# A fifth buffer for the unsplit weights of a two-layer decoder trunk, with three tiles moved into shared buffers

## The chip, the core and the metric

The kernel runs as one program on one core of a Trainium2 chip. Its time is the device time of one execution in microseconds (us). Five engines run side by side, each through its own instructions in a fixed order, and wait for each other through semaphores: TensorE (PE, matrix products into PSUM, with weight loads shown apart as PEld), VectorE (DVE), ScalarE (ACT), GpSimd (POOL) and SyncE (SP). DMA transfers are issued from the instruction streams of SP, POOL and ACT. An instruction whose semaphore isn't there yet holds up everything behind it on the same engine.

## The reference, cut to what matters

The input is 512 positions of 1024 channels, all numbers float32. Two layers follow each other; each is a mixer and a gated feed-forward block (FFN), both added to the residual `h`.

```python
def gated_conv_ffn(x, w_gate, w_up, conv_w, conv_b, w_down):
    g = jnp.einsum('bsd,df->bsf', x, w_gate)
    g = causal_dwconv3(g, conv_w) + conv_b
    up = jnp.einsum('bsd,df->bsf', x, w_up)
    return jnp.einsum('bsf,fd->bsd', jax.nn.silu(g) * up, w_down)

def reference(x, ...):
    h = x
    for layer in range(2):
        xn = rms_norm(h, norm_mix[layer])
        if layer == 0:   # projections to 2048 channels; gated convolution, causal pooling
            mix = concat(short_gated_conv(...), multiscale_pool(z, w_pool, pool_scale))
            h = h + mix @ w_out_even
        else:            # gelu(xn @ w_in_odd) = u, v; mixing of positions in chunks of 128
            h = h + chunked_spatial_gating(u, v, sgu_norm, w_spatial, b_spatial) @ w_out_odd
        hn = rms_norm(h, norm_ffn[layer])
        h = h + gated_conv_ffn(hn, ...)        # 1024 -> 2816 -> 1024
    return rms_norm(h, final_norm)
```

## The kernel before

**Products and their weights.** PE multiplies float32 data in three products (`mm3`, L133 to L135): both factors are split into a rounded part `hi` and a rest `lo`, and hi by hi, hi by lo and lo by hi are added in PSUM. So every block of weights goes through three tiles. The first is `raw`, 128 x 1024 float32 (512 KB), which a DMA on SP's queue fills from memory; then come `whi` and `wlo`, which the products read. `parts` (L125) makes them with one ACT copy (L128) and one DVE subtraction (L129). `summed` (L116) makes `wlo` without DVE: ACT writes minus the raw block into it (L120) and a DMA issued by POOL adds the raw block in place (L121). All raw blocks share the pool tag `raw` with four buffers; `whi` and `wlo` have six each. A raw buffer can be loaded again when all its readers are through, a `summed` block's DMA among them.

**The FFN.** The 2816 hidden channels are 22 tiles of 128, worked off in pairs f = 0, 2, 4, ... 20. From f = 4 on, `both(f)` computes the gate and the up projection of two tiles by a scheme with seven half-size products in place of eight, which needs sums of weight blocks. It takes four raw blocks, here called `g0`, `u0`, `g1` and `u1` of the pair: gate and up weights of the first and the second half of the 1024 input channels. L653, L654, L659 and L660 (DVE) form the sums `s12` and `s34` from them; L653 reads both halves (`g0` and `g1`, or `u0` and `u1`). Lines 633 and 634 split `a11` and the sums; `g1` and `u1` go through `summed`. PE then runs 14 groups of 12 products (L624) in a written order (L695 to L697); their results leave PSUM by ACT copies (L682) and DVE additions (L687, L692) into `rows` and `kept`. L692 after product 7 also frees the bank that product 3 then adds into. The convolution follows (`conv`: L505 on ACT, two L507 on DVE into a tile `c`), then silu (L513), the product with the up projection (L703, L704, L707) and the split of the activation into `a_hi` (L247) and `a_lo` (L249). After the pairs listed in `PARTS` (f = 0 and 2; 4; 6 and 8; 10 and 12; 14 and 16; 18 and 20) a down projection adds to the output: `project` with blocks `d` in layer 0 (results taken by L292), blocks `dn` in layer 1 (L922). It too takes four raw blocks per part. "Boundary 8 to 10" below is the place where the down projection of the part that ends with pair 8 is followed by pair 10.

**What sets the order.** The source says which work there is and what depends on what. A scheduler puts the instructions of each engine in order when the program is built, from modelled durations, and hands out the buffers; so a changed buffer count also moves instructions. On the chip the order is fixed. SP issues the raw loads in the order in which the blocks are used: `g0`, `u0`, `g1`, `u1` of a pair, then the blocks of the next pair or of the down projection. With four buffers, the load of a block waits for the readers of the block four places ahead of it in that list; and a load that waits holds up those behind it in SP's queue.

**The tiles that the change moves.** `wpl` holds the pooling weights of mixer 0 (L425), `g_bc` the norm gain of the spatial unit of mixer 1 (L751), and `c` the convolution of the FFN (L504, two buffers of its own). The tag `sq` of the pool `tp` (two buffers) holds squares for the norms. `fin`, the last norm's gain, already shares the tag `raw` (L899).

Of the kernel before, what the change touches and what calls it, by code (L numbers as in the profile page):

```python
# [8 lines left out]
F32 = mybir.dt.float32  # L9
# [6 lines left out]
P = 128  # L16
D = 1024
S = 512
# [12 lines left out]
def tile_trunk(ctx: ExitStack, tc: tile.TileContext, x, norm_mix, norm_ffn, final_norm,  # L31
# [8 lines left out]
    wp = ctx.enter_context(tc.tile_pool(name="wp", bufs=1))  # L40
    tp = ctx.enter_context(tc.tile_pool(name="tp", bufs=2))
# [3 lines left out]
    def mm_bank(name):  # L45
        return ps_mm.tile([P, 512], F32, tag="mm", name=name)
# [59 lines left out]


    def fetch(src, a, b, name):
        raw = wp.tile([P, a, b], F32, tag="raw", bufs=4, name=f"raw_{name}")
        nc.sync.dma_start(raw, src)  # L110
        return raw, a, b, name

    def weights(src, a, b, name):
        return parts(*fetch(src, a, b, name))
# [108 lines left out]
    def newton(ms, n, name, r):  # L223


        sd = work("sd", n, name)
        nc.scalar.activation(sd, ms, AF.Sqrt)
        nc.vector.reciprocal(r, sd)
        nc.vector.tensor_tensor(ms, ms, r, ALU.mult)
        nc.vector.scalar_tensor_tensor(ms, ms, -0.5, r, op0=ALU.mult, op1=ALU.mult)  # L230
# [71 lines left out]
    def in_fetch(name, w, c0, k, n):  # L302
        return fetch(w[k * P : (k + n) * P, c0 : c0 + 512].rearrange("(k p) c -> p k c", p=P),
                     n, 512, f"{name}_{k}")
# [28 lines left out]
    def mixer0():  # L333
        nonlocal prm0
        w = w_in_even[0]
        with tc.tile_pool(name="m0", bufs=1) as mp:
# [85 lines left out]
            in_group("z", w, 1536, True, z_done, 2, zchunks, ahead)  # L422
            prm0 = params0()

            wpl = mp.tile([P, 4, P], F32, name="wpl")  # L425
            nc.sync.dma_start(wpl, w_pool[0].rearrange("g c d -> c g d"))
            wpl_hi = mp.tile([P, 4, P], F32R, name="wpl_hi")
            wpl_lo = mp.tile([P, 4, P], F32R, name="wpl_lo")
# [59 lines left out]
    class Ffn:  # L488
# [12 lines left out]

        def conv(self, t, ft):
            ap, prm, n = self.ap, self.prm, f"{self.layer}_{ft}"
            c = ap.tile([P, S], F32, tag="c", bufs=2, name=f"c{n}")  # L504
            nc.scalar.activation(c, t[:, 0:S], AF.Copy, scale=prm("cf", ft))  # L505
            for i in (1, 2):
                nc.vector.scalar_tensor_tensor(c, t[:, i : S + i], prm("cf", i * NF + ft), c,  # L507
                                               op0=ALU.mult, op1=ALU.add)
            return c
# [9 lines left out]
        def pair_weights(self, f, order, by_dma=""):  # L519

            ch = {}
            for key, half in order:
                name = f"{key}{self.layer}_{f}_{half}"
                raw = wp.tile([P, 4, 2 * P], F32, tag="raw", bufs=4, name=f"raw_{name}")
                w = (w_ffn_gate if key == "g" else w_ffn_up)[self.layer][:, f * P : (f + 2) * P]
                w = w.rearrange("(h k p) c -> p h k c", h=2, p=P)
                for h_ in range(2):
                    nc.sync.dma_start(raw.rearrange("p (k h) c -> p h k c", h=2)[:, h_],
                                      w[:, h_, 2 * half : 2 * half + 2])
                ch[key, half] = (summed if key in by_dma else parts)(raw, 4, 2 * P, name)  # L530
            return ch
# [216 lines left out]
    def mixer1(norm):  # L748
        w = w_in_odd[0]
        with tc.tile_pool(name="m1", bufs=1) as mp:  # L750
            g_bc = mp.tile([P, 1, D], F32, name="g_bc")  # L751
            nc.scalar.dma_start(g_bc, sgu_norm.rearrange("(o l) d -> o l d", o=1)
                                .to_broadcast([P, 1, D]))
            ws = mp.tile([P, NK, P], F32, tag="v", bufs=4, name="ws")
# [117 lines left out]
    def ffn1(norm):  # L872
        with tc.tile_pool(name="f1", bufs=1) as ap:
            def sums(kp):
                return [cp.tile([P, 2, HALF], F32R, tag=f"h{k}", name=f"t23_{k}")
                        for k in (kp, kp + NP)]

            ffn = Ffn(1, prm1, norm, ap, sums)
            acts = ffn.acts
            y = [ap.tile([P, D], F32, name=f"y{t}") for t in range(NT)]  # L880
            ssf = ap.tile([P, NT, PAD], F32, name="ssf")[:, :, :2]

            def turn_residual(t, half):
                ps = mm_bank(f"hT{t}_{half}")
                for i in range(4):
                    nc.tensor.transpose(ps[:, i * P : (i + 1) * P],
                                        h[half * 4 + i][:, t * P : (t + 1) * P], ident)
                nc.scalar.copy(y[t][:, half * 512 : (half + 1) * 512], ps)

            def before(i, j):  # L890
                if i < 2:
                    turn_residual(j, i)

            for groups, a, b in PARTS:
                for f in groups:
                    ffn.hidden(f, before=before)
                last = b == NF
                if last:
                    fin = wp.tile([P, D], F32, tag="raw", bufs=4, name="fin")  # L899
                    nc.scalar.dma_start(  # L900
                        fin, final_norm.rearrange("(o d) -> o d", o=1).to_broadcast([P, D]))
                    root = small[:, 2:3]
                    nc.scalar.activation(root, eps, AF.Sqrt)
                ch = {}
                for ft in range(a, b):
                    ch[ft] = weights(w_ffn_down[1][ft * P : (ft + 1) * P, :]
                                     .rearrange("(k p) c -> p k c", p=P), 1, D, f"dn1_{ft}")

                def lhs(ft, j):
                    ts_ = slice((j // 2) * P, (j // 2 + 1) * P)  # L910
                    return acts[ft][0][:, ts_], acts[ft][1][:, ts_]

                def rhs(ft, j):
                    c = slice((j % 2) * 512, (j % 2 + 1) * 512)
                    return ch[ft][0][:, 0, c], ch[ft][1][:, 0, c]

                yf = {}

                def done(j, ps):
                    t, half = j // 2, j % 2  # L920
                    dst = y[t][:, half * 512 : (half + 1) * 512]
                    nc.vector.tensor_tensor(dst, ps, dst, ALU.add)  # L922
                    if not last:
                        return
                    sq = tp.tile([P, S], F32, tag="sq", name=f"sqf{j}")
                    ss = ssf[:, t, half : half + 1]
                    nc.scalar.activation(sq, dst, AF.Square, accum_out=ss)
                    yf[half] = ap.tile([P, S], F32, tag="s", bufs=3, name=f"yf{j}")
                    nc.vector.tensor_tensor(yf[half], dst, fin[:, half * 512 : (half + 1) * 512],
                                            ALU.mult)  # L930
                    if half == 0:
                        nc.vector.tensor_scalar(ss, ss, 1.0 / D, EPS, op0=ALU.mult, op1=ALU.add)
                        return
                    ms = ssf[:, t, 0:1]
                    nc.vector.scalar_tensor_tensor(ms, ss, 1.0 / D, ms, op0=ALU.mult, op1=ALU.add)
                    r = tp.tile([P, LINE], F32, tag="rc", name=f"rc_fin{t}")[:, :1]
                    newton(ms, 1, f"fin{t}", r)
                    nc.vector.tensor_scalar(ms, ms, 1.5, None, op0=ALU.add)
                    for c in range(2):
                        cs = slice(c * 512, (c + 1) * 512)  # L940
                        nc.vector.tensor_scalar(y[t][:, cs], yf[c], r, ms,
                                                op0=ALU.mult, op1=ALU.mult)
                        nc.sync.dma_start(out[t * P : (t + 1) * P, cs], y[t][:, cs])

                group8(f"dn{a}", list(range(a, b)), lhs, rhs, 4, done)

    def group8(name, ks, lhs, rhs, tail, on_done):
        banks = {}
        head = max(0, len(ks) - tail)
        order = [(i, j) for i in range(head) for j in range(8)]  # L950
        order += [(i, j) for j in range(8) for i in range(head, len(ks))]
        for i, j in order:
            if j not in banks:
                banks[j] = mm_bank(f"{name}_{j}") if j < 7 else aux_bank(f"{name}_{j}")
            mm3(banks[j], lhs(ks[i], j), rhs(ks[i], j), i == 0, i == len(ks) - 1)
            if i == len(ks) - 1:
                on_done(j, banks[j])

    n = mixer0()
    n = ffn0(n)  # L960
    n = mixer1(n)
    ffn1(n)


# [28 lines left out]
```

## Time and profile before

| | |
|---|---|
| median of 3 runs | 1007.23 us (1005.27 to 1007.35) |
| profiled execution, its own time | 1007.18 us |
| span of the profile, first to last instruction | 1005.5 us |
| granted TensorE clock, mean | 0.996 |
| PE busy | 988.0 us (98% of the span) |
| DVE busy | 699.3 us (70%) |
| ACT busy | 521.9 us (52%) |
| POOL busy | 100.8 us (10%) |
| moved by DMA | 124.53 MB, mean 124 GB/s |

The profile was taken of one execution; its span lies 1.7 us below that execution's own time. Groups of instructions go by line, engine and tile names, with buffer numbers left out: `s12g` is the sum for the gate weights of any pair. In a timeline each row gives the start, the time, the engine, line and operation, and in square brackets how long the engine had been idle and what ended it. SPq, POOLq and ACTq are the queues on which those engines issue DMAs. In the view of the waits each row gives who waited, for whom, and then the total in us, how many times and the longest.

### The profile page before, as it was taken

How to read it: one execution, taken by the hardware profiler on the slowest of the kernel's cores; microseconds unless marked ns; L12 is line 12 of the kernel's file. 1: busy time of each engine (PE TensorE's matmuls, PEld its weight loads, DVE VectorE, ACT ScalarE, POOL GpSimd, SP SyncE). 2: the span in 40 equal slices, each digit the busy share in tenths (PEclk: the TensorE clock that was granted, in tenths of full speed). 3: DMA queues.
4: the chain of work that ended last, by engine and by line, in shares of the span. 5: the costliest groups of instructions: out<-in, count | busy, mean ns of one | idle time of the engine just before them, and what ended most of it. 6: DMA issues, size and time to landing. Idle time of an engine off the chain costs nothing.

```text
span 1005.5 us, 14738 instructions
## 1 busy us (share of the span) xinstructions
PE 988.0 (98%) x5835; PEld 875.6 (87%) x5835; DVE 699.3 (70%) x1057; ACT 521.9 (52%) x775; POOL 100.8 (10%) x117
## 2 busy tenths in 40 slices
PE   8999999999999999999999999999999999999997
PEld 6788888898999989899888888888999899898895
DVE  5877457968776786867933545399667867687577
ACT  5622345744653746537655443675446366363563
POOL 2132020300000000000300001211000010000100
PEclk9999999999999999999999999999999999999999
DMA  6522224454454545545433222445446465454532
GB/s 222 191 96 92 85 84 126 105 150 123 129 147 129 162 113 132 147 115 167 134 118 105 74 93 91 98 97 132 129 105 156 117 142 152 102 152 125 123 109 83
DMA packets 81905, 124.53 MB, mean 124 GB/s; under 512 B 4293, under 2 KB 53677, under 8 KB 81837
## 3 DMA queue, kind: packets, MB, share of 16 engines
q1 hardware_dynamic: 73580, 98.96, 31.1%
q0 software_dynamic: 6912, 23.07, 12.5%
q10 hardware_dynamic: 1344, 1.58, 0.5%
q8 instruction: 45, 0.74, 0.3%
q14 instruction: 24, 0.19, 0.1%
HBM read 98.42 MB, written 2.10 MB: 100 GB/s over the span
## 4 chain that ended last, share of the span: by engine, by line
PE 81%; issue 7%; DMA 5%; DVE 5%; ACT 2%; POOL 0%; SPq 0%; ACTq 0%; DVEq 0%; POOLq 0%
PE gu L133 3%; PE gu L134 3%; PE gu L135 3%; PE d L133 3%; PE d L134 3%; PE d L135 3%; PE dn L133 2%; PE dn L135 2%; PE dn L134 2%; DMA raw_g<-in_w_ffn_gate_dram 2%; PE u L135 1%; PE oo L135 1%; PE u L134 1%; PE oo L133 1%; PE u L133 1%
## 5 line engine op out<-in xcount | busy, mean ns | idle before, releaser
L507 DVE SCALAR_TENSOR_TENSOR c<-rows,prm,c 128x512 f32<-128x512 f32 x88 | 67.7, 792 | 4.4 <-ACT c L505 4.1
L134 PE MATMUL d<-a_lo,whi_d 128*128 128x512 f32 x176 | 68.6, 390 | 0.0
L133 PE MATMUL dn<-whi_dn,a_hi 128*128 128x512 f32 x176 | 68.6, 390 | 0.0
L134 PE MATMUL dn<-wlo_dn,a_hi 128*128 128x512 f32 x176 | 68.6, 390 | 0.0
L135 PE MATMUL d<-a_hi,wlo_d 128*128 128x512 f32 x176 | 68.5, 389 | 0.0
L135 PE MATMUL dn<-whi_dn,a_lo 128*128 128x512 f32 x176 | 67.3, 390 | 0.0
L133 PE MATMUL d<-a_hi,whi_d 128*128 128x512 f32 x176 | 66.9, 390 | 0.0
L121 POOL DMA_DIRECT2D wlo_g<-raw_g x22 | 19.1, 868 | 382.1 <-ACT wlo_g L120 315.9
L922 DVE TENSOR_TENSOR y<-dn,y 128x512 f32<-128x512 f32 x48 | 32.3, 686 | 22.8 <-PE dn L135 22.3
L120 ACT ACTIVATE wlo_g<-raw_g 128x1024 fp32r<-128x1024 f32 x22 | 23.2, 1055 | 42.4 <-PE dn L134 42.4
L129 DVE TENSOR_TENSOR wlo_u<-raw_u,whi_u 128x1024 fp32r<-128x1024 f32 x16 | 19.6, 1224 | 34.2 <-ACT whi_u L128 34.1
L513 ACT ACTIVATE s<-c,prm 128x512 f32<-128x512 f32 x44 | 30.8, 716 | 21.5 <-DVE c L507 21.5
L633 ACT ACTIVATE whi_s12u<-s12u 128x1024 fp32r<-128x1024 f32 x18 | 18.9, 1049 | 43.2 <-PE d L134 33.8
L633 ACT ACTIVATE whi_s12g<-s12g 128x1024 fp32r<-128x1024 f32 x18 | 19.1, 1061 | 41.7 <-DVE s12g L654 36.1
L129 DVE TENSOR_TENSOR wlo_dn<-raw_dn,whi_dn 128x1024 fp32r<-128x1024 f32 x22 | 26.8, 1221 | 19.0 <-ACT whi_dn L128 19.0
L135 PEld LDWEIGHTS dn<-whi_dn,a_lo 128*128 128x128 f32 x176 | 33.0, 188 | 7.5 <-DVE a_lo L249 0.2
L134 PEld LDWEIGHTS d<-a_lo,whi_d 128*128 128x128 f32 x176 | 33.0, 188 | 7.3 <-DVE a_lo L249 0.2
L133 PEld LDWEIGHTS dn<-whi_dn,a_hi 128*128 128x128 f32 x176 | 33.0, 188 | 7.1 <-ACT a_hi L247 0.2
L129 DVE TENSOR_TENSOR wlo_d<-raw_d,whi_d 128x1024 fp32r<-128x1024 f32 x22 | 26.8, 1221 | 17.9 <-ACT whi_d L128 17.9
L133 PEld LDWEIGHTS d<-a_hi,whi_d 128*128 128x128 f32 x176 | 32.8, 188 | 7.1
L292 DVE TENSOR_TENSOR h<-d,h 128x512 f32<-128x512 f32 x48 | 32.5, 685 | 9.3 <-PE d L135 9.3
L135 PEld LDWEIGHTS d<-a_hi,wlo_d 128*128 128x128 f32 x176 | 33.0, 188 | 6.8
(1201 smaller groups left out, 3423.4 us busy)
## 6 DMA issues: line engine op xcount, KB each, us to landing
raw_g<-in_w_ffn_gate_dram SPq DMA_DIRECT2D x36, 512.0 KB, 4.1
raw_u<-in_w_ffn_up_dram SPq DMA_DIRECT2D x36, 512.0 KB, 4.5
wlo_g<-raw_g POOLq DMA_DIRECT2D x22, 512.0 KB, 4.6
raw_d<-in_w_ffn_down_dram SPq DMA_DIRECT2D x22, 512.0 KB, 3.6
raw_dn<-in_w_ffn_down_dram SPq DMA_DIRECT2D x22, 512.0 KB, 3.5
wlo_u<-raw_u POOLq DMA_DIRECT2D x18, 512.0 KB, 4.6
raw_oe<-in_w_out_even_dram SPq DMA_DIRECT2D x8, 512.0 KB, 3.6
raw_g<-in_w_ffn_gate_dram SPq DMA_DIRECT2D x16, 256.0 KB, 2.8
```

What stands on the lines that cost most here:

```text
L120: nc.scalar.activation(lo, raw, AF.Copy, scale=-1.0)
L121: nc.gpsimd.dma_start(lo, raw, accum_op=ALU.add)
L129: nc.vector.tensor_tensor(lo, raw, hi.bitcast(F32), ALU.subtract)
L133: nc.tensor.matmul(ps, lhs[0], rhs[0], start=start, stop=False)
L134: nc.tensor.matmul(ps, lhs[0], rhs[1], start=False, stop=False)
L135: nc.tensor.matmul(ps, lhs[1], rhs[0], start=False, stop=stop)
L292: nc.vector.tensor_tensor(h[k], ps, h[k], ALU.add)
L507: nc.vector.scalar_tensor_tensor(c, t[:, i : S + i], prm("cf", i * NF + ft), c, op0=ALU.mult, op1=ALU.add)
L513: nc.scalar.activation(s, c, AF.Silu, bias=self.prm("bf", ft))
L633: nc.scalar.activation(hi, src, AF.Copy)
L922: nc.vector.tensor_tensor(dst, ps, dst, ALU.add)
```

## The change

The tag `raw` gets a fifth buffer (4 KB per partition). To make room, the convolution's tile `c` moves from its own two buffers to the two of the tag `sq`, and `wpl` and `g_bc` become users of the tag `raw`: each holds one of the five buffers for the time that it is in use. No instruction is added or dropped.

```diff
     def fetch(src, a, b, name):
-        raw = wp.tile([P, a, b], F32, tag="raw", bufs=4, name=f"raw_{name}")
+        raw = wp.tile([P, a, b], F32, tag="raw", bufs=5, name=f"raw_{name}")
         nc.sync.dma_start(raw, src)
...
-            wpl = mp.tile([P, 4, P], F32, name="wpl")
+            wpl = wp.tile([P, 4, P], F32, tag="raw", bufs=5, name="wpl")
             nc.sync.dma_start(wpl, w_pool[0].rearrange("g c d -> c g d"))
...
-            c = ap.tile([P, S], F32, tag="c", bufs=2, name=f"c{n}")
+            c = tp.tile([P, S], F32, tag="sq", name=f"c{n}")
             nc.scalar.activation(c, t[:, 0:S], AF.Copy, scale=prm("cf", ft))
...
-                raw = wp.tile([P, 4, 2 * P], F32, tag="raw", bufs=4, name=f"raw_{name}")
+                raw = wp.tile([P, 4, 2 * P], F32, tag="raw", bufs=5, name=f"raw_{name}")
...
-            g_bc = mp.tile([P, 1, D], F32, name="g_bc")
+            g_bc = wp.tile([P, 1, D], F32, tag="raw", bufs=5, name="g_bc")
             nc.scalar.dma_start(g_bc, sgu_norm.rearrange("(o l) d -> o l d", o=1)
                                 .to_broadcast([P, 1, D]))
...
-                    fin = wp.tile([P, D], F32, tag="raw", bufs=4, name="fin")
+                    fin = wp.tile([P, D], F32, tag="raw", bufs=5, name="fin")
```

In the built program the fifth buffer moves instructions on every engine but POOL. In the FFN of both layers the changes are these, pair by pair:

- At the boundaries 8 to 10, 12 to 14 and 16 to 18, `s12g` and the first part of `s34g` of the next pair (L653, L659 on DVE) stood behind the last `a_lo` of the current pair; now they stand ahead of L687 `rows`, behind L692 `kept` of the current pair, with the whole convolution behind them.
- At the boundary 4 to 6, L653, L659, L654 and L660 for the gate stand around L692 `kept` of pair 4 in the same way.
- Between two pairs of one part (6 to 8, 10 to 12, 14 to 16, 18 to 20), `s12u` of the second pair (L653) moves ahead of the splits of `a11` (L634) or of other work, a few places.
- On PE, at the boundaries 8 to 10, 12 to 14 and 16 to 18, the down projection's first products with the current pair's `a_hi` come five places earlier, and those with its `a_lo` three places earlier.

## The prediction

> **What bounds the kernel now.** I read the page first, then the waits of PE, then the timelines around the longest of them and around the places where the built program differs.
>
> ```profile
> PE 988.0 (98%) x5835; PEld 875.6 (87%) x5835; DVE 699.3 (70%) x1057; ACT 521.9 (52%) x775; POOL 100.8 (10%) x117
> PE g_18e L624 <- DVE rows L692: 3.0, 2, 2.4
> PE g_6e L624 <- DVE rows L692: 1.1, 1, 1.1
> PE u_10a L624 <- ACT kept L682: 1.0, 1, 1.0
> PE g_10e L624 <- DVE rows L692: 0.3, 1, 0.3
> ```
>
> PE is busy for 98% of the span, so a change can save little and lose much: whatever makes PE wait is added to the time. The four rows of waits are all of PE's waiting in the FFN, 5.4 us. Who kept DVE from L692? The longest case, pair 18 of layer 1 (PE, then DVE, then SP's and POOL's queues):
>
> ```profile
> 948.68 0.28 PE L624 MATMUL g_18a<-t,wlo_g 128*128 128x256 f32 x1
> 951.41 0.39 PE L624 MATMUL g_18e<-hgh,whi_s34g 128*128 128x256 f32 x1 [2.44 <-DVE rows L692]
> ...
> 944.58 0.42 DVE L687 TENSOR_TENSOR rows<-g_18b,rows 128x256 f32<-128x256 f32 x1
> 949.19 0.69 DVE L653 TENSOR_TENSOR s12u<-raw_u,raw_u 128x512 f32<-128x512 f32 x1 [4.20 <-DMA raw_u<-in_w_ffn_up_dram]
> 950.93 0.42 DVE L692 TENSOR_TENSOR rows<-g_18e,rows 128x256 f32<-128x256 f32 x1
> ...
> 936.69 0.37 SPq L110 DMA_DIRECT2D raw_g<-in_w_ffn_gate_dram  x1
> 944.27 0.37 SPq L110 DMA_DIRECT2D raw_u<-in_w_ffn_up_dram  x1
> ```
>
> DVE stood 4.20 us at L653 for a raw block whose load SP had issued only at 944.27, and L692 was queued behind it. These waits come from the buffers. The other place to read is a boundary between parts, here 8 to 10 in layer 0 (DVE, ACT, PE, SP; then the time to landing of the third load at this boundary, at 16 to 18 in layer 0 and at 12 to 14 in layer 1):
>
> ```profile
> 283.43 0.42 DVE L692 TENSOR_TENSOR kept<-u_8e,kept 128x256 f32<-128x256 f32 x1 [1.42 <-ACT kept L682]
> 285.43 1.23 DVE L129 TENSOR_TENSOR wlo_d<-raw_d,whi_d 128x1024 fp32r<-128x1024 f32 x1 [1.58 <-ACT whi_d L128]
> 287.24 0.42 DVE L687 TENSOR_TENSOR rows<-g_8e,rows 128x256 f32<-128x256 f32 x1
> 294.10 0.68 DVE L249 TENSOR_TENSOR a_lo<-s,a_hi 128x512 fp32r<-128x512 f32 x1
> 294.70 0.68 DVE L653 TENSOR_TENSOR s12g<-raw_g,raw_g 128x512 f32<-128x512 f32 x1
> 293.01 0.63 ACT L247 ACTIVATE a_hi<-s 128x512 fp32r<-128x512 f32 x1 [0.51 <-DVE s L707]
> 293.82 0.62 PE L133 MATMUL d<-a_hi,whi_d 128*128 128x512 f32 x2
> 280.06 0.42 SPq L110 DMA_DIRECT2D raw_g<-in_w_ffn_gate_dram  x1
> 280.57 0.46 SPq L110 DMA_DIRECT2D raw_u<-in_w_ffn_up_dram  x1
> DMA to landing us min/median/max: 6.1/6.1/6.1
> DMA to landing us min/median/max: 5.8/5.8/5.8
> DMA to landing us min/median/max: 6.9/6.9/6.9
> ```
>
> Here PE is served with nothing to spare: `a_hi` ends at 293.64 (293.01 + 0.63), PE takes it at 293.82; `a_lo` ends at 294.78, and PE takes it 0.18 later too. It is so at all eight boundaries with a convolution ahead of a down projection. A delay of the convolution there is a delay of PE.
>
> **Part 1: the gain between pairs of one part.** With five buffers `u1` of the second pair no longer waits for the landing of `wlo_u` but for that of `wlo_g`, one place earlier. At pair 18, layer 1, that is when SP issues `raw_g` now: 936.69. At 4.9 us (what the load at 944.27 took, by DVE's start at 949.19) it lands at 941.6. From there the changed order of DVE is L653, L634 twice, L654, L687, L634 `wlo_s12g`, L659, L692. At the steps between starts in the rows (0.6 for 512 elements, 0.34 for 256, 1.14 for 1024) L692 would end near 947; with the ACT copy that `wlo_s12g` waits for (now until 945.2, some 0.6 later since the issue of `fin` on ACT's queue now waits for another landing) near 948. PE wants it at 948.75. The wait goes. The same holds at pair 6 (`u1` released at 746.6 in place of 754.1), pair 10 and pair 18 of layer 0. What they are worth is read from the starts of PE's products, 0.12 apart otherwise: 450.60 to 451.47, 758.56 to 759.91, 819.31 to 820.61, 823.46 to 823.99 and 948.68 to 951.41. Less 0.12 each that is 6.2 us, and the step behind each is 0.1 longer: 6.7. At pair 10 the block still lands only near 817, and L692 comes out just in time; I leave 0.4 there. Gain **6.3 us**, ends 4 and 6.7.
>
> **Part 2: the loss at the boundaries.** The scheduler now puts L653 and L659 of the next pair directly behind L692 `kept`, which ends at 283.85, and ahead of the whole convolution. Is `g1` there by then? SP's queue, by the releasers in the built program: `g0` waits for the landing of `wlo_u` of pair 8, which releases the second `raw_d` now, at 279.60; `u0` and `g1` stand behind it, and their buffers are free at 278.86 and 280.32 (ends of L129 `wlo_d`). So `g0`, `u0`, `g1` go out at about 279.6, 280.1 and 280.6: the pattern in which `raw_d`, `raw_g`, `raw_u` go out now, whose third load takes 6.1 us here. `g1` lands at 286.7, and DVE stands 2.8 us with the convolution behind it. Worked on with the rows' steps: L653 286.7, L659 287.3, L687 287.9, L129 288.2, four L507 from 289.4 (the last ends 292.1), L687, L703, L704 to 293.1; on ACT the second silu until 292.9; L707 293.0 to 293.7; ACT `a_hi` 293.7 to 294.35; L129, then `a_lo` twice, to 296.0. Without the block's lateness L687 would wait for PE's product 3 and `a_hi` would come at 292.6. PE's new order asks for it five products of 0.227 earlier, at 292.69. So PE waits 1.7 us (with 0.05 for the semaphore, from L692's end at 951.35 to PE's start at 951.41), and 0.1 for `a_lo`, wanted seven products later: **1.8 us**. In general the cost is the landing less 284.9, that is less 1.05 behind the end of L692 `kept`.
>
> The other five, by their L692 ends (346.06, 408.33; 779.75, 843.84, 906.24) and the starts of the third load now (343.23, 405.05; 776.59, 840.33, 902.84), with 5.8 and 6.9 where the view gives the landing and the middle value 6.1 where it doesn't: 2.2, 1.5; 1.9, 2.35, 1.65. Sum with the first **11.4 us**. All at 5.8 it would be 9.1, all at 6.9 it would be 15.7; a load alone takes 4.1 (median on the page), and then nothing is lost. I take the trios' rows, since three loads in a row are what the new queue issues.
>
> At 4 to 6 four operations (2.4 us) go ahead of the convolution, DVE is idle for 1.6 us of it today, and PE takes one other product first (0.23): 0.5 us, twice, **1.0**; ends 0 and 1.6.
>
> **Part 3: the moved tiles.** `c` has two buffers as before; squares are written before the first and after the last convolution of an FFN. `wpl` is loaded at 14.58 as now, since its buffer is free at 7.3. ACT's split of `ac_6` goes ahead of L368 at 32.13, but its load, released at 24.4, lands near 28. `g_bc` waits on ACT's queue for `wlo_u` of pair 20 (issued at 462.18 on POOL, 4.6 to land: 466.8), behind an L682 that ends then: no wait; were that landing 2 us late, L682 at 467.60 would be too, which PE's order covers. The wait for `ws` (0.5 on PE) may go or stay. I count 0, ends -0.7 and +1.
>
> **Sum.** -6.3 + 11.4 + 1.0 = +6.1 us on the profiled execution's 1007.18, which lies at the median of 1007.23: **1013 us**.
>
> **The rivals.** *The third load lands early (faster).* Nothing is lost at the six boundaries if `g1` lands by 284.9, 4.3 us behind its issue; then -6.3 + 1.0 gives 1002. The sum changes its sign where the third load takes 5.2 us. For it: loads alone take 4.1. Against it: 5.8, 6.1 and 6.9 in the trios. The Trainium skill (DMA: Bandwidth & Descriptors, Anatomy of one DMA) gives a DMA a fixed 2.0 us plus its bytes at 436 GB/s, a fit for DMAs issued by GpSimd. By it three blocks of 512 KB land 5.6 us behind the first issue, 285.2, and by my estimate of the other boundaries from that the change would come out near 1004; the three rows above say 1.2 to 2.2 us more. The Trainium skill (Perfetto Trace Analysis, Optimization Strategy) also reads a gap that repeats on the busiest engine as a sign of too few buffers, which part 1 bears out and part 2 doesn't.
>
> *Both sides cancel.* Losses of 4.3 to 8.3 us in place of 12.4, from shorter waits (third load at 5.2 to 5.5) or from ACT and DVE catching up: 1005 to 1009. Against it: the chain from L653 to `a_hi` has no idle time to catch up in.
>
> *The gain doesn't come.* If `u1` lands late all the same, since it now runs beside POOL's `wlo_u` transfer (one took 7.3 us at 936.82), part 1 is 0 and the time 1019.6. Against it: DVE has 1.1 us to spare at pair 6 and 0.7 at pair 18.
>
> **How the numbers follow.** The forecast 0.68 (own range 1010 to 1018), faster 0.12, cancel 0.10, no gain 0.10. About 0.2% is what a measurement here can tell from no change. So faster 0.12, within 0.2% 0.10, slower 0.78. The range reaches from 1003.5 into the faster case to 1018, and leaves out most of the last case.
>
> **What would show it.** In the changed profile DVE `s12g` L653 should wait some 2 to 3.5 us for `raw_g` at six places (14 to 20 us in all; the 20.6 us for `raw_u` mostly gone), PE should wait for ACT `a_hi` L247 in `d` and `dn`, 1.5 to 2.4 us each, and the waits for L692 and L682 should be gone. It is wrong if L653 doesn't wait at the boundaries, or if PE still waits for L692.

## The result, and the profile after

The changed kernel takes 1018.59 us (median of 4 runs, 1016.45 to 1019.20) beside 1006.25 us for the kernel before on the same chip: a ratio of 1.0117 with a 95% interval of 1.0097 to 1.0137, or some 12 us more. The forecast was slower, by 6 us, to 1013 us with a range up to 1018. The direction was right, the forecast size was half of what came, and the time lies just outside the range.

PE's waits in the changed kernel, by who waited for whom (total, times, longest):

```profile
PE d L133 <- ACT a_hi L247: 6.4, 4, 2.2
PE dn L133 <- ACT a_hi L247: 6.4, 4, 2.1
PE wst L763 <- POOL ws L756: 2.1, 1, 2.1
...
PE g_10e L624 <- DVE rows L692: 0.9, 1, 0.9
```

The waits for L692 and L682 that made up the FFN's waiting before are gone but for one, at pair 10 of layer 1: 0.9 us, where the prediction had left 0.4 and had named a wait for L692 as a sign that it is wrong (the second profile of the changed kernel doesn't have it). In their place PE waits for `a_hi` at all eight boundaries, 12.8 us, and the wait for `ws` has grown from 0.5 to 2.1 us. Who keeps ACT from `a_hi`? The waits of DVE for the blocks, first before and then in the changed kernel, and DVE's timeline in the changed kernel at the boundary 8 to 10 of layer 0, with ACT's and PE's rows:

```profile
DVE s12u L653 <- DMA raw_u<-in_w_ffn_up_dram: 20.6, 7, 4.7
...
DVE s12g L653 <- DMA raw_g<-in_w_ffn_gate_dram: 17.9, 8, 5.0
```

```profile
DVE s12g L653 <- DMA raw_g<-in_w_ffn_gate_dram: 32.6, 11, 3.5
...
DVE s12u L653 <- DMA raw_u<-in_w_ffn_up_dram: 9.0, 4, 4.6
```

```profile
283.85 0.42 DVE L692 TENSOR_TENSOR kept<-u_8e,kept 128x256 f32<-128x256 f32 x1 [1.42 <-ACT kept L682]
286.91 0.69 DVE L653 TENSOR_TENSOR s12g<-raw_g,raw_g 128x512 f32<-128x512 f32 x1 [2.64 <-DMA raw_g<-in_w_ffn_gate_dram]
...
288.46 1.22 DVE L129 TENSOR_TENSOR wlo_d<-raw_d,whi_d 128x1024 fp32r<-128x1024 f32 x1
289.59 2.73 DVE L507 SCALAR_TENSOR_TENSOR c<-rows,prm,c 128x512 f32<-128x512 f32 x4
...
293.42 1.17 ACT L247 ACTIVATE a_hi<-s 128x512 fp32r<-128x512 f32 x2 [0.34 <-DVE s L704]
292.89 0.39 PE L135 MATMUL d<-a_hi,wlo_d 128*128 128x512 f32 x1
294.64 0.73 PE L133 MATMUL d<-a_hi,whi_d 128*128 128x512 f32 x2 [1.37 <-ACT a_hi L247]
```

Of the 32.6 us, 17.7 stand at the six boundaries where the prediction expected 14 to 20, and 4.9 at the two of 4 to 6, where it named none. This is the picture that the prediction drew: L653 stands directly behind L692 `kept`, waits 2.64 us for the third load of a trio, and the convolution starts later by that much (its first L507 5.7 us behind the start of L692, where it was 3.1). The load is this one (start and time of the issue on SP's queue; the second row is the time from the issue to the landing):

```profile
280.99 0.46 SPq L110 DMA_DIRECT2D raw_g<-in_w_ffn_gate_dram  x1
DMA to landing us min/median/max: 5.8/5.8/5.8
```

It landed at 286.8, within 0.1 us of the forecast. So the mechanism is the forecast one; what the profile doesn't settle is how much of the 12 us it carries.

PE's wait here has two parts. Counted from the start of L692 `kept`, the last `a_hi` ended after 10.2 us in the kernel before (283.43 to 293.64) and ends after 10.7 us in the changed kernel (283.85 to 294.59). So only 0.5 us of DVE's 2.64 reach `a_hi`: the second L129 and a split of `a11` (L634), which stood ahead of L707, now stand behind it. The other part, 1.1 us, is PE's own new order: PE asks for `a_hi` 9.3 us behind the start of L692 (one product behind 292.89), where it took it 10.4 us behind that start before. The prediction counts with both: had `g1` been there in time, by its working `a_hi` would have come at 292.6, early enough for PE's earlier asking at 292.69. No run has the new orders of DVE and PE with an early load, so that last point is worked out and not shown.

### The profile page after: what moved, and what is told of

Read it like the earlier page. It is cut to its first block, busy times and chain, and to the rows that moved or that the text cites. A ratio compares the mean times of both kernels' runs of the same rounds, so it can differ in the third digit from the quotient of the medians.

```text
span 1017.2 us, 14726 instructions
## 1 busy us (share of the span) xinstructions
PE 989.9 (97%) x5835; PEld 875.5 (86%) x5835; DVE 700.8 (69%) x1057; ACT 522.3 (51%) x775; POOL 100.9 (10%) x117
## 3 DMA queue, kind: packets, MB, share of 16 engines
q10 hardware_dynamic: 1344, 1.58, 0.4%
## 4 chain that ended last, share of the span: by engine, by line
PE 80%; DVE 9%; DMA 7%; ACT 2%; issue 1%; SPq 0%; POOL 0%; DVEq 0%; ACTq 0%; POOLq 0%
DMA raw_g<-in_w_ffn_gate_dram 5%; PE d L133 3%; PE dn L133 3%; PE d L134 3%; PE d L135 3%; PE dn L134 3%; PE gu L133 3%; PE dn L135 3%; PE gu L135 3%; PE gu L134 3%; DVE c L507 2%; PE u L133 1%; PE u L135 1%; PE oo L133 1%; PE oo L134 1%; PE oe L135 1%
## 5 line engine op out<-in xcount | busy, mean ns | idle before, releaser
L507 DVE SCALAR_TENSOR_TENSOR c<-rows,prm,c 128x512 f32<-128x512 f32 x88 | 66.1, 792 | 6.6 <-ACT c L505 6.5
L129 DVE TENSOR_TENSOR wlo_u<-raw_u,whi_u 128x1024 fp32r<-128x1024 f32 x16 | 19.6, 1223 | 34.2 <-ACT whi_u L128 34.1
L134 PEld LDWEIGHTS dn<-wlo_dn,a_hi 128*128 128x128 f32 x176 | 33.4, 190 | 6.7
L505 ACT ACTIVATE c<-rows,prm 128x512 f32<-128x512 f32 x44 | 31.0, 719 | 10.1 <-DVE rows L687 9.5
```

Of the source, the lines that this page charges most:

```text
L129: nc.vector.tensor_tensor(lo, raw, hi.bitcast(F32), ALU.subtract)
L134: nc.tensor.matmul(ps, lhs[0], rhs[1], start=False, stop=False)
```

## The experiments

Four theories are set against each other. **A**: DVE's queue is the cause. The scheduler put sums of the next pair ahead of the convolution, where they wait for a load. **B**: the shared tiles cost the time (`c` in `sq`, `wpl` and `g_bc` in `raw`). **C**: more transfers at once make the loads slower. **D**, a variant of A: the sums delay the convolution by their own time, not by the load that they wait for. Ratios are to the kernel before in the same batch of runs, with 95% intervals; 0.1% is 1.0 us.

### The changed kernel again

No edit.

> The changed kernel once more, to see which of its gaps recur. Theory A (the scheduler put the sums of the next pair ahead of the convolution, and DVE stands there for a late load): the eight waits of PE for a_hi come back, 1.3 to 2.3 us each, 12 to 14 us in all, and the wait for wst with about 2 us. The half clock that the profile showed from 864 to 867 us (0.56 and 0.59, about 1.5 us of time) is not of the order of instructions and may lie elsewhere or be absent. Theory B (the shared tiles, c in sq, wpl and g_bc in raw, cost the time) and theory C (more transfers at once make loads slower) say the same for this run; it is the base for the others. About 1018 us for all.

Measured: 1018.28 us, ratio 1.0127 (1.0113 to 1.0141). The waits for `a_hi` are there again (5.5 us in layer 0, 6.0 in layer 1, eight in all), and `wst` again with 2.1. The half clock that the first profile has near 864 us (the last section) is not.

### The sums back behind the convolution

```diff
+        def behind(self, f, key, add):
+            if key == "g" and f in (6, 10, 14, 18):
+                tc.add_manual_dep(add.ins, a_lo[0].ins.name, mybir.DependencyInfo(
+                    mybir.DependencyClass.NoSync, mybir.DependencyReason.DATA),
+                    reason="s12g behind a_lo")
...
-            nc.vector.tensor_tensor(lo, src, hi.bitcast(F32), ALU.subtract)
+            a_lo[0] = nc.vector.tensor_tensor(lo, src, hi.bitcast(F32), ALU.subtract)
...
-                nc.vector.tensor_tensor(s12[:, 0], r0[:, :, P:], r1[:, :, P:], ALU.add)
+                self.behind(f, key, nc.vector.tensor_tensor(s12[:, 0], r0[:, :, P:], r1[:, :, P:], ALU.add))
```

> The changed kernel with one thing undone: at the four boundaries of each layer the first sum of the next pair (L653 for the gate) is put behind the last a_lo on DVE's queue, where it stood before. Buffers, moved tiles and SP's queue are those of the changed kernel. Theory A: the waits for a_hi go (15 us with the steps behind them), the gain between pairs stays (about 5.5 us), the earlier wst still costs 1.6: 1002 to 1004.5 us, that is 2 to 4 us faster than before. Theory B: c still shares sq and the loss stays, about 1018. Theory C: the loads are issued as early as in the changed kernel, so their slowness stays and with it more than half of the loss, 1012 or more.

Measured: 1002.62 us, ratio 0.9978 (0.9967 to 0.9988), 15 us less than the changed kernel and faster than before. Behind the first 30 us PE waits only for this:

```profile
PE wst L763 <- POOL ws L756: 2.1, 1, 2.1
...
PE g_10e L624 <- DVE rows L692: 0.3, 1, 0.3
```

The first row is mixer 1; the second is all that is left in the FFN. Theory A holds. B falls as a cause of the loss at the boundaries, and so does C taken by itself: five buffers and shared tiles are as in the changed kernel, and at 8 to 10 SP still issues `g0`, `u0` and `g1` within 1.0 us. But the one dependency moves more than L653: the scheduler also puts the splits back, and PE takes `a_hi` 10.4 us behind the start of L692 again, as before. So the run takes back the new order of DVE and that of PE together.

### The moves alone

```diff
-        raw = wp.tile([P, a, b], F32, tag="raw", bufs=5, name=f"raw_{name}")
+        raw = wp.tile([P, a, b], F32, tag="raw", bufs=4, name=f"raw_{name}")
... (the same for the other users of the tag)
```

> The three tiles are moved as in the changed kernel, but the tag raw keeps four buffers. Its order is that of before on DVE, ACT, SP and POOL; on PE the transposes wst stand 12 products earlier. Theory A: no boundary loss, no gain between pairs, only the earlier wst, +1.0 to +1.6 us: 1006.5 to 1008.5. Theory B: most of the loss is here, 1015 or more. Theory C: as before, 1006 to 1007.

Measured: 1008.31 us, ratio 1.0035 (1.0023 to 1.0048): 3.5 us slower, over twice the 1.0 to 1.6 that I expected of the earlier `wst`. Its order differs from that of before in one place (on DVE and ACT too, against what the expectation says): ACT issues the loads of `g_bc` and `ws` earlier, and `wst` and its splits move forward with them. PE and POOL there, first before, where POOL waits for the landing of `ws`, and then in the changed kernel:

```profile
505.98 0.66 PE L763 MATMUL wst<-ident,ws 128*128 128x128 f32 x4 [0.55 <-POOL ws L756]
504.83 1.09 POOL L756 TENSOR_SCALAR_AFFINE_SELECT ws<-ws 128x1024 f32<-128x1024 f32 x1 [1.57 <-DMA ws<-in_w_spatial_dram]
```

```profile
507.77 0.39 PE L134 MATMUL v<-wlo_v,hgh 128*128 128x512 f32 x1
510.25 0.55 PE L763 MATMUL wst<-ident,ws 128*128 128x128 f32 x3 [2.10 <-POOL ws L756]
```

```profile
507.33 1.37 POOL L189 TENSOR_TENSOR ssq_m<-ssq_m,sq_m 128x512 f32<-128x512 f32 x1 [0.85 <-ACT sq_m L188]
508.65 1.55 POOL L756 TENSOR_SCALAR_AFFINE_SELECT ws<-ws 128x1024 f32<-128x1024 f32 x1
```

POOL's order is that of before, so L756 runs behind the last square sum however early `ws` lands. PE comes to `wst` 12 products (2.7 us) earlier in its own order and waits.

### That wait taken away, with and without the rest

```diff
-            for q in range(2):
+            def turn_ws(q):
...
-            in_group("v0", w, 1024, False, v_done(0), 2)
+            in_group("v0", w, 1024, False, v_done(0), 2, before=lambda k: turn_ws(k - 3) if k in (3, 4) else None)
```

This edit was added to the kernel with the sums put back, to the kernel with the moves alone, and to the changed kernel.

> As the run that put L653 back behind a_lo (1002.62 us, 0.9978 of before), and besides the two groups of transposes wst are issued on PE behind 36 products of v in place of 20; before had 32. If the wait of PE for ws (2.1 us, a step of 2.27 more than a product) comes only from PE asking 12 products of 0.227 = 2.7 us too early, it goes, and with it the half clock that two profiles showed behind it (about 1.5 us in those executions): 999.5 to 1001.3 us, 0.4% to 0.5% faster than before. If ws is late for another reason and moves along, 1002 to 1003.

> Four buffers for raw, the three tiles moved, and wst issued on PE behind 36 products of v: the run with the moves alone (1008.31 us) without its early wst. The other pair of runs gave 4.15 us for that place (1002.62 to 998.47). If the moves cost nothing but the place of wst, 1003.5 to 1005.5 us, the time of before or a little less (before itself waits 0.8 us for ws). If the shared buffers cost something of their own (c in sq, wpl and g_bc in raw), 1006.5 or more.

> The changed kernel with wst behind 36 products of v and nothing else: the eight waits for a_hi stay. If the place of wst costs here what it costs without them, 2.3 to 4.2 us less than the changed kernel (1018.3 to 1018.6): 1014 to 1016 us. If the waits of PE further up leave slack there, so that it costs less beside them, 1017 or more.

Measured, in this order: 998.47 us, ratio 0.9931 (0.9918 to 0.9944); 1004.99 us, ratio 0.9994 (0.9984 to 1.0004); 1014.78 us, ratio 1.0088 (1.0072 to 1.0103). The place of `wst` is worth 4.1, 3.3 and 3.5 us in the three by the medians (1002.62, 1008.31 and 1018.28 without the edit), and 4.7, 4.1 and 3.9 us by the ratios, which set each run against the kernel before in its own batch. With it mended the moves cost nothing that can be measured, so theory B is down to this one place on PE's queue. The first of the three came out 1 us below its expected range. PE's wait is 2.3 us of that; in two profiles a lower clock behind the wait adds 1.6 (the last section), and the rest is open. The first of the three is faster than both kernels. The row of the engines' busy time on its page, whose span is 996.7 us, and all of PE's waits:

```profile
PE 986.3 (99%) x5835; PEld 875.3 (88%) x5835; DVE 699.3 (70%) x1057; ACT 521.0 (52%) x775; POOL 100.8 (10%) x117
```

```profile
PE clock L56 <- DVE idle L53: 1.3, 1, 1.3
PE z L134 <- DVE hgl L370: 0.8, 1, 0.8
PE z L133 <- ACT hgh L368: 0.5, 1, 0.5
PE xt_ps L357 <- DMA xt<-in_x_dram: 0.4, 1, 0.4
```

All four lie in the first 30 us; PE waits nowhere in either FFN.

### The sums ahead, but without the wait

```diff
-                nc.vector.tensor_tensor(s12[:, 0], r0[:, :, P:], r1[:, :, P:], ALU.add)
+                self.behind(f, key, nc.vector.tensor_tensor(s12[:, 0], r0[:, :, P:], (r0 if key == "g" and f in (6, 10, 14, 18) else r1)[:, :, P:], ALU.add))
```

`behind` holds L653 behind L692 `kept` here.

> The sums stay ahead of the convolution, as in the changed kernel, but do not wait: at the eight boundaries L653 of the gate adds the second half of g0 to itself in place of that of g1, so that the sums of these pairs are not those of the reference; L653 is held directly behind L692 kept, and the scheduler puts L653, L659 and also L654 there (three sums, 1.8 us, where the changed kernel has two). PE asks for a_hi at the place of before, one product later. Theory A (the landing of g1 is what costs): DVE stands idle for 1.58 us there anyway until the copy whi_d, so the sums cost 0 to 0.3 us at each boundary: 1002.5 to 1005 us. Rival D (the sums' own time ahead of the convolution costs, the load only little): 1.2 to 1.8 us at each of eight boundaries stay, 1012 to 1017 us.

Measured: 1002.06 us, ratio 0.9967 (0.9954 to 0.9979), 0.4 us below the expected range and the time of the kernel with the sums put back. DVE at 8 to 10, first with the sums ahead and no wait, then with the sums put back:

```profile
281.97 0.42 DVE L692 TENSOR_TENSOR kept<-u_8e,kept 128x256 f32<-128x256 f32 x1 [1.42 <-ACT kept L682]
282.31 0.68 DVE L653 TENSOR_TENSOR s12g<-raw_g 128x512 f32<-128x512 f32 x1
282.91 0.68 DVE L659 TENSOR_TENSOR s34g<-raw_g 128x512 f32<-128x512 f32 x1
283.51 0.68 DVE L654 TENSOR_TENSOR s12g<-s12g,raw_g 128x512 f32<-128x512 f32 x1
284.11 1.22 DVE L129 TENSOR_TENSOR wlo_d<-raw_d,whi_d 128x1024 fp32r<-128x1024 f32 x1
```

```profile
281.97 0.42 DVE L692 TENSOR_TENSOR kept<-u_8e,kept 128x256 f32<-128x256 f32 x1 [1.42 <-ACT kept L682]
283.97 1.23 DVE L129 TENSOR_TENSOR wlo_d<-raw_d,whi_d 128x1024 fp32r<-128x1024 f32 x1 [1.58 <-ACT whi_d L128]
```

Three sums fit into the 1.58 us that DVE waits for `whi_d` anyway and put L129 back by 0.14 us. Theory D falls: it is the landing of `g1`, not the sums. (The splits and PE's asking stand about as before here, so this run too differs from the changed kernel in more than the wait.)

### The load of g1 earlier, and later

```diff
-            raws = ffn_weights(layer, f, [(key, half) for half in range(2) for key in "gu"])
+            raws = ffn_weights(layer, f, [("g", 0), ("g", 1), ("u", 0), ("u", 1)])
```

> The four blocks of a pair are loaded in the order g0, g1, u0, u1 in place of g0, u0, g1, u1; nothing else is changed by hand. The scheduler now puts all four sums of the gate ahead of the convolution and L653 even ahead of L692, but PE asks for a_hi as late as in the kernel before. Theory A: g1 lands about 1.4 us earlier (second of the three loads, 4.9 to 5.1 us behind the first issue), which is still behind DVE; with two more sums (1.24) and L692 (0.34) behind the wait, and 1.13 of room given back on PE, some 0.6 to 1.3 us are lost at each of six boundaries and little at 4 to 6: 1008 to 1012 us, with shorter waits of L653 (1 to 2 us) for raw_g. Theory B: unchanged, about 1018. Theory C: unchanged, since as many loads are in the air, 1016 or more.

Measured: 1015.53 us, ratio 1.0101 (1.0087 to 1.0115). The direction was right, the size was not: PE still waits 1.1 to 2.1 us at each of the six boundaries, 9.5 in all (not at 4 to 6). Since PE asks for `a_hi` as late as before in this run, such a loss doesn't need PE's earlier asking. DVE at 8 to 10 here:

```profile
283.08 0.69 DVE L653 TENSOR_TENSOR s12g<-raw_g,raw_g 128x512 f32<-128x512 f32 x1 [2.87 <-DMA raw_g<-in_w_ffn_gate_dram]
283.69 0.42 DVE L692 TENSOR_TENSOR kept<-u_8e,kept 128x256 f32<-128x256 f32 x1
...
290.27 1.22 DVE L129 TENSOR_TENSOR wlo_d<-raw_d,whi_d 128x1024 fp32r<-128x1024 f32 x1
291.41 0.42 DVE L703 TENSOR_TENSOR s<-kept,s 128x256 f32<-128x256 f32 x1
```

The load did come earlier: L653 starts 5.3 us behind the first issue of the trio (277.75) where the changed kernel has 6.9. But it waits longer (2.87 us) than the 1 to 2 us that I expected, since it now asks ahead of L692. My working had counted the two sums more and L692 behind the wait; I had not seen that the scheduler also put the second L129 (1.14 us) ahead of L703, where it stands in front of `a_hi`.

Then the other way round:

```diff
-            raws = ffn_weights(layer, f, [(key, half) for half in range(2) for key in "gu"])
+            raws = ffn_weights(layer, f, [("g", 0), ("u", 0), ("u", 1), ("g", 1)])
```

> The four blocks of a pair are loaded in the order g0, u0, u1, g1, so that g1 comes last; nothing else is changed by hand. Since its model now has g1 late, the scheduler itself puts the gate's sums behind the convolution and a_lo, and PE's order is that of the run that put L653 back. Theory A: the time comes from that order, so the later load makes the kernel faster: g1 is issued where u1 is issued in the changed kernel (289.7, landing 293.5 at 8 to 10) and DVE asks at 294.7: 1002 to 1004 us. Theory C (late loads or too many of them cost as such): no better than the changed kernel, 1015 or more.

Measured: 1002.64 us, ratio 0.9970 (0.9958 to 0.9981). Loading the block later made the kernel some 1.5% faster than the changed one, with no dependency added by hand. That is the same time as with the sums put back, and theory C by itself has no room left: that the third load of a trio is slow (5.8 us) counts only through an instruction that waits for it ahead of the convolution.

### The boundary 4 to 6 by itself

The edit of the second experiment, with `f in (6,)`.

> As the run that put L653 back behind a_lo, but only at 4 to 6 in both layers; the other six boundaries stay as in the changed kernel. It sizes the boundary 4 to 6, which the prediction put at 0.5 us each and the profiles show at 1.3 to 1.8 with 0.1 behind: 2.6 to 3.4 us less than the changed kernel, 1015 to 1016; if it were worth 0.5 each, 1017.5. Six waits for a_hi of 1.5 to 2.3 us stay.

Measured: 1014.60 us, ratio 1.0089 (1.0073 to 1.0104), some 3.8 us below the changed kernel run again by the ratios, and 0.4 us below the range that I expected. By these runs 4 to 6 costs nearly four times the forecast 1.0 us. DVE there, in the changed kernel and with the sums put back:

```profile
221.01 0.69 DVE L653 TENSOR_TENSOR s12g<-raw_g,raw_g 128x512 f32<-128x512 f32 x1 [2.70 <-DMA raw_g<-in_w_ffn_gate_dram]
221.62 0.69 DVE L659 TENSOR_TENSOR s34g<-raw_g 128x512 f32<-128x512 f32 x1
222.22 0.42 DVE L692 TENSOR_TENSOR kept<-u_4e,kept 128x256 f32<-128x256 f32 x1
...
223.88 1.22 DVE L129 TENSOR_TENSOR wlo_d<-raw_d,whi_d 128x1024 fp32r<-128x1024 f32 x1
```

```profile
219.71 0.42 DVE L692 TENSOR_TENSOR kept<-u_4e,kept 128x256 f32<-128x256 f32 x1 [1.42 <-ACT kept L682]
221.71 1.23 DVE L129 TENSOR_TENSOR wlo_d<-raw_d,whi_d 128x1024 fp32r<-128x1024 f32 x1 [1.58 <-ACT whi_d L128]
```

L653 stands ahead of L692 `kept` here, and it too waits for `g1` (2.70 us). L129 comes 2.17 us later. PE's step at `a_hi` is 1.78 us longer than a product there, since PE asks one product (0.23) later; in layer 1 it is 1.28. The two profiles of the changed kernel show 3.1 and 2.6 us for the two layers together; the rest of the 3.8 is within what the ratios can tell.

## Why the forecast had the right sign and the wrong size

The runs form a chain in which one step is taken at a time, so the terms can be read as differences of ratios (each good to about 2 us):

| step | forecast | measured |
|---|---|---|
| the tiles moved (before to moves alone) | 0, ends -0.7 and +1 | +3.5 |
| fifth buffer, sums in the place of before (moves alone to sums put back) | -6.3 | -5.7 |
| sums ahead, and PE asking earlier, at six boundaries (to the kernel with 4 to 6 put back) | +11.4 | +11.2 |
| sums ahead at 4 to 6, twice (to the changed kernel run again) | +1.0, ends 0 and 1.6 | +3.8 |
| sum | +6.1 | +12.8 (the first measurement: 1.0117) |

**Part 1, the gain**, held. Mended in the place of `wst`, the fifth buffer is worth 0.9994 to 0.9931, 6.3 us. The waits of L653 for `raw_u` fell from 20.6 to 9.0 us, where the prediction had them mostly gone (in layer 0 three waits for `raw_g` between pairs of a part grew from 4.2 to 10.0 us meanwhile, and PE waits for neither there), and the waits for L692 at pairs 6 and 18 are gone.

**Part 2 at six boundaries** held, within 0.3 us at each. PE's steps at the six waits in the profile of the changed kernel are longer than a product by 1.52, 2.31, 1.46, 1.85, 2.29 and 1.62 us, 11.1 in all. The forecast was 1.8, 2.2, 1.5, 1.9, 2.35 and 1.65. The mechanism held with the number: L653 starts behind the end of L692 `kept` within 0.2 us of the forecast landing at each of the six. It came from taking the landing out of trios of loads (5.8 to 6.9 us) and not from the page's 4.1, which the prediction calls that of a load alone and which is the median of all loads of the group: the third load took 5.8 us at 8 to 10 and 5.7 at 16 to 18. The rival in which the load lands early gains only below 5.2 and is out. The Trainium skill (DMA: Bandwidth & Descriptors, Anatomy of one DMA) would have three such blocks landed 5.6 us behind the first issue by my estimate from its fit; in the changed kernel the first issue of this trio is at 279.98 and the third block lands at 286.8, 6.8 us behind it. The measurement decides: with 5.6 us the forecast would have been about 1004, a small gain.

**Part 2 at 4 to 6** is the first step that failed: the term of 0.5 us, twice, with ends of 0 and 1.6 for the sum, where PE's steps show 2.6 to 3.1 us and the runs 3.8. I wrote that four operations of 2.4 us go ahead and that DVE's idle 1.6 us take up part of them. I counted operations and never asked when their load lands, which I had done at the other six. SP issues this `g1` at 215.84, and L653 waits until 221.01, 1.3 us after the point at which L692, now queued behind it, could have run (219.71).

**Part 3, the moves,** is the second: the term 0 with an upper end of 1, in the sentence "The wait for `ws` (0.5 on PE) may go or stay", where the runs show +3.5. I had looked at the loads of the moved tiles and at PE's order only at the boundaries. With the tiles moved, PE's `wst` moved 12 products forward, to ahead of what it waits for. (Of the three tiles `g_bc` is the one that is loaded here; the runs don't move them one by one.) The wait can then cost more than its length (below). Of the 6.7 us that the forecast lacked, 3.5 are here and 2.8 at 4 to 6.

The rivals: cancelling didn't come, as argued. (Its bounds don't fit each other: a third load at 5.2 to 5.5 us gives losses of 6.5 to 8.3 us by the prediction's own sum, and 4.3 would need 4.8.) "The gain doesn't come" was wrong, though its time of 1019.6 was the nearest to what came; that is luck, since the gain came, and other losses took its place.

## What to carry to other kernels

A further buffer does what it promises to the waits for it (here 6 us), but where a scheduler places instructions, it also lets consumers of the new early loads move ahead of older work on an in-order queue. So read the built order of every engine, PE and the parts far from the change too, and ask of each instruction that moved forward when the data it waits for really lands, behind how many other loads. If the order is the loss, it can be put back by itself: fifth buffer, old order and `wst` in place gave 998.47 us, 0.7% below the kernel before.

## What was unexpected of the hardware

A wait of some 2 us can cost 3.9. From the start of the first product of `v` to that of the last, PE takes 46.0 us in the kernel before, 45.2 us in the three profiles in which it doesn't wait for `ws`, 47.5 us in six of the eight with the wait of 2.1 us, and 49.1 us in the other two. In these two the wait is followed by products at half rate: 0.43 us from start to start in place of 0.227. Here with the sums put back; the columns are the window, its length, busy time and count of PE, PEld, DVE, ACT and POOL, then the granted clock, the DMA share and GB/s:

```profile
500.00:503.00 3.00, 0.89 (x6) 0.47 (x5) 3.00 (x2) 0.52 (x1) 2.58 (x2) 0.97 0.47 175
503.00:506.40 3.40, 3.40 (x11) 2.68 (x10) 1.35 (x2) 1.64 (x2) 0.00 (x0) 0.52 0.39 137
```

In the changed kernel's profile the same stands behind one wait for `a_hi`:

```profile
861.00:864.00 3.00, 0.87 (x4) 0.41 (x3) 3.00 (x7) 2.15 (x4) 0.00 (x0) 1.00 0.26 91
864.00:868.00 4.00, 4.00 (x13) 3.11 (x12) 2.42 (x5) 0.00 (x0) 0.00 (x0) 0.57 0.44 131
```

Away from the start and the end of the kernel, the twelve profiles have a half clock in six places, each time for 3.4 us and each time behind a wait of PE of 1.8 to 2.3 us, most of which lies in the 3.4 us just ahead of it. It costs some 1.5 us (up to eight products, 0.2 us more each). It follows some such waits and not others: the same wait for `a_hi` near 860 in the changed kernel run again (2.0 us) has a clock of 1.00 behind it. The Trainium skill (TensorE: Matmul & The Clock Gate, Part 1) describes this: the clock is halved after an idle window of about 3.4 us, and the windows run free of the kernel. The rows agree in the half rate, in the 3.4 us and in that it comes in some executions and not in others, but here waits of 1.8 to 2.3 us were enough; what decides between them the runs don't show.

The lower clock doesn't explain all that the place of `wst` costs. With 2.3 us for the wait and 1.6 us in two executions of eight, it would be 2.7 us on average by my estimate; the runs say 3.3 to 4.7, each good to about 2 us. What the rest is, if there is one, stays open.
